# A two-layer decoder trunk on one core: the convolution's shifted copies are begun on GpSimd's queue instead of ScalarE's

## The chip, the cores and the metric

The kernel runs on one core of a Trainium2 chip. The core has five engines that run side by side, each with its own instruction queue worked off in order: TensorE (PE in the profile; its weight loads are PEld), VectorE (DVE), ScalarE (ACT), GpSimd (POOL) and SyncE (SP). ScalarE, GpSimd and SyncE can begin transfers (DMAs); the transfers themselves run on the core's 16 DMA engines. The metric is the device time of one execution in microseconds (us); lower is better.

## The reference, cut to what matters

Two decoder layers work on 256 tokens of 1024 numbers in float32. Layer 0 mixes a convolution group of 768 channels and a memory attention of 4 heads, then a dense SwiGLU; layer 1 mixes sliding-window attention and the memory attention, then 8 experts of which each token uses 2. The change lies in the convolution of layer 0:

```
a    = proj[..., :CONV_CH] + b_glu[:CONV_CH]
gate = proj[..., CONV_CH:2 * CONV_CH] + b_glu[CONV_CH:]
u = a * jax.nn.sigmoid(gate)
u_pad = jnp.pad(u, ((0, 0), (CONV_WIDTH - 1, 0), (0, 0)))
c = lax.conv_general_dilated(u_pad, dw_w[:, None, :], window_strides=(1,), padding='VALID',
    dimension_numbers=('NWC', 'WIO', 'NWC'), feature_group_count=CONV_CH) + dw_b
c = jax.nn.silu(layer_norm(c, ln_g, ln_b))
```

Each of the 768 channels is convolved along the tokens with its own 31 taps. The layer norm runs over all channels, so nothing behind it can start before the last channel is done.

## The kernel before, in words

The 768 channels are six blocks of 128 (c = 0 to 5). For each block TensorE makes the two halves of the input projection (`pa`, `pg`, lines 98 to 100), ScalarE the sigmoid (L393), VectorE the product `u` (L394), and ScalarE's queue writes `u` of the block to a DRAM buffer `ud` (L395).

The convolution is done on TensorE. A block's channels are cut into four groups of 32 (q = 0 to 3). For each group a transfer (L461) reads `ud` so that the 128 partitions of a tile `sh` hold 32 channels at four shifts of 0 to 3 tokens: 4 x 32 rows of 288 floats, 144 KB. GpSimd builds `bands` (L457), diagonal matrices of the taps, one buffer for each of two blocks in turn. Then 32 matmuls (8 tap groups g, each with q = 0, 1, 2, 3 in turn; L466) add up the block in the one PSUM buffer `pcv`, and ScalarE moves it to `cv` (L468). In the trace each of these matmuls is two records, so that x64 is a block.

`sh` has six buffers and a block takes four. So the first two copies of a block have buffers while the block before is still being multiplied, and the last two (q = 2, 3) can only be begun when the matmuls that read q = 0 and 1 of the block before are done. I call the start of such a pair a hand-over; there is one into each of blocks 1 to 5.

Between these stand other pieces of work that TensorE takes up meanwhile: the transposes `xt` and the matmuls `pkv` of the memory's keys and values, the memory query `pmq` (2 x 24 matmuls), transposes of heads `ht`, and the four rounds of memory attention: scores `sc`, softmax on VectorE and ScalarE (`nm`, `pr`), transposes `pt`, output `mo`. The heads are normed first: VectorE sums squares (`hss`), GpSimd makes the factor (`ms`, `rs`, lines 150 and 151), VectorE applies it (`kn`, `qn`), and TensorE's `ht` needs that. After block 5 come the layer norm (`pmean`, `pst`, `pbc`) and the output projection `wo`, and then the dense SwiGLU, layer 1 and the experts.

Weights are loaded on SyncE's queue into a small ring of buffers; a load begins when its buffer has been used up. The order of the instructions on each engine is worked out before the run by a scheduler that plays the program through with durations of its own, except for TensorE's order in the experts' stage, which is written out by hand. So a change of a transfer's queue can move instructions on other engines too.

```
sh = [wk0.tile([P, UW - 4], F32, name="sh", tag="sh", bufs=6) for _ in range(4)]
for q in range(4):
    act.dma_start(sh[q], bass.AP(tensor=ud.tensor, ...
```

Of the kernel before, what the change touches and what calls it, by code (L numbers as in the profile page):

```python
# [47 lines left out]
def hybrid_kernel(  # L48
# [7 lines left out]
    act, dve, pool, pe, sp = nc.scalar, nc.vector, nc.gpsimd, nc.tensor, nc.sync  # L56
# [81 lines left out]
    def col(name, k=0):  # L138
        return cols[:, offs[name] + k:offs[name] + k + 1]
# [27 lines left out]
    with ExitStack() as ph:  # L167
# [5 lines left out]
        def bank(tag, name):  # L173

            if tag in ("mm", "tp"):
                return psb.tile([P, 512], F32, name=name, tag=tag)
            return psx[-1].tile([P, 512], F32, name=name, tag=tag,
                                bufs=dict(sc=2, cv=1, o=1, acc=4, so=1)[tag])
# [167 lines left out]
        ud = dram.tile([NCT, P, UW], F32, name="ud")  # L346
# [35 lines left out]
        for i in range(3):  # L382
            wa, wg = [halves(m, pool if (i, j) in LOWPOOL else None, after=None)
                      for j, m in enumerate(win[2 * i:2 * i + 2])]
            for j in range(2):
                c = 2 * i + j
# [16 lines left out]
        for name, n, f in (("memg", KD, 32.0), ("ffg", KD, 32.0), ("swg", KD, 32.0),  # L403
                           ("hmk", 1, 8.0), ("hsk", 1, 8.0)):
            c = cols[:, offs[name]:offs[name] + n]
# [49 lines left out]
        for c in range(NCT):  # L455
            T = bands[:, c % 2]
            pool.tensor_tensor(T, eye4[:, None, None, :].to_broadcast([P, GT, 4, 32]),  # L457
                               w4[:, :, 4 * c:4 * c + 4, None].to_broadcast([P, GT, 4, 32]), op=OP.mult)
            sh = [wk0.tile([P, UW - 4], F32, name="sh", tag="sh", bufs=6) for _ in range(4)]
            for q in range(4):  # L460
                act.dma_start(sh[q], bass.AP(tensor=ud.tensor, offset=ud[c, 32 * q, 0:1].offset,  # L461
                                                  ap=[[1, 4], [UW, 32], [1, UW - 4]]))
            pcv = bank("cv", "pcv")[:, :S]
            for g in range(GT):
                for q in range(4):
                    pe.matmul(pcv[q * 32:(q + 1) * 32, :], T[:, g, q, :], sh[q][:, 4 * g:4 * g + S],  # L466
                              start=(g == 0), stop=(g == GT - 1), tile_position=(0, q * 32))
            act.activation(cv[:, c, :], pcv, AF.Identity, bias=col("dwb", c))  # L468
# [192 lines left out]
    with ExitStack() as ph:  # L661
# [99 lines left out]
        for kk in range(KD // 2):  # L761
# [6 lines left out]
            for k in range(2 * kk, 2 * kk + 2):  # L768
                q = k % 4
# [401 lines left out]
```

## Time and profile before

| what | value |
|---|---|
| median of 3 runs | 1364.86 us (1364.3 to 1366.51) |
| the profiled execution's own time | 1362.78 us |
| its span, first to last instruction | 1361.1 us |
| PE, PEld | 1286.2 us (94%), 720.4 us (53%) |
| DVE, ACT, POOL | 387.5 us (28%), 298.7 us (22%), 70.7 us (5%) |

Times in rows are microseconds from the span's start. The profiled execution is 1.7 us longer than its span and 2.08 us under the median. A row such as "[3.81 <-DMA sh<-ud]" says that the engine was idle for 3.81 us ahead of this instruction until a transfer into `sh` had landed. ACTq and SPq rows are the time that a queue spent on issuing a transfer, not the transfer itself. [...]

### The profile page before, as it was taken

What the parts mean: (1) busy time and instruction counts of PE and PEld (TensorE: products, weight loads), DVE (VectorE), ACT (ScalarE), POOL (GpSimd) and SP (SyncE); (2) the same over time, 40 slices, a digit from 0 to 9 for tenths busy, and PEclk for the clock granted to TensorE, in tenths of its full rate; (3) what the DMA queues carried; (4) which work ended last, traced back from release to release, by engine and by line L of the source; (5) the groups of instructions that cost most, each with busy time, mean ns of one, the idle gap of its engine ahead of it and who ended that gap; (6) DMA issues with size and microseconds to landing.
All of it is one profiled execution on the core that took longest, in us unless ns stands there. A gap on an engine that the chain in (4) does not pass through costs nothing. (4 is left out here: it accounts for less than half of the span.)

```text
span 1361.1 us, 19725 instructions
## 1 busy us (share of the span) xinstructions
PE 1286.2 (94%) x7908; PEld 720.4 (53%) x7908; DVE 387.5 (28%) x782; ACT 298.7 (22%) x575; POOL 70.7 (5%) x110
## 2 busy tenths in 40 slices
PE   6978799999898879999999999999999999999997
PEld 5844589999775643344454343444343454434443
DVE  5633465555466421012112111111110211100212
ACT  6333354444365300001111000011000111000111
POOL 4220200000031200000000000000000000000000
PEclk9989899999898988999999999999999999999999
DMA  9842145555472467989999999999999999999994
GB/s 291 291 132 72 63 149 198 184 184 184 124 223 83 191 230 299 363 336 394 413 409 409 409 412 404 409 410 412 409 409 404 411 409 408 412 411 409 403 411 199
DMA packets 137445, 420.87 MB, mean 309 GB/s; under 512 B 9658, under 2 KB 43256, under 8 KB 125048
## 3 DMA queue, kind: packets, MB, share of 16 engines
q1 hardware_dynamic: 133016, 414.39, 79.1%
q10 hardware_dynamic: 4320, 4.96, 1.1%
q8 instruction: 77, 1.26, 0.4%
q14 instruction: 32, 0.26, 0.1%
HBM read 417.37 MB, written 1.95 MB: 308 GB/s over the span
## 5 line engine op out<-in xcount | busy, mean ns | idle before, releaser
L926 PE MATMUL pa<-raw,xe 128*64 128x512 f32 x1024 | 269.8, 599 | 6.6 <-DVE hx L942 4.0
L926 PE MATMUL pb<-raw,xe 128*64 128x384 f32 x1024 | 213.2, 488 | 0.0
L982 PE MATMUL py<-raw,hT 128*64 128x512 f32 x896 | 199.3, 595 | 4.0 <-PEq L1023 1.6
L926 PEld LDWEIGHTS pb<-raw,xe 128*64 128x64 f32 x1024 | 81.1, 138 | 140.4 <-issue 140.4
L91 DVE TENSOR_TENSOR wlo<-raw,whi 128x1024 fp32r<-128x1024 f32 x108 | 131.9, 1260 | 80.8 <-ACT whi L90 80.8
L982 PEld LDWEIGHTS py<-raw,hT 128*64 128x64 f32 x896 | 67.5, 137 | 131.9 <-issue 121.4
L926 PEld LDWEIGHTS pa<-raw,xe 128*64 128x64 f32 x1024 | 77.5, 137 | 104.2 <-issue 70.0
L90 ACT CAST whi<-raw 128x1024 fp32r<-128x1024 f32 x112 | 111.5, 1046 | 54.5 <-issue 26.2
L934 PE MATMUL po<-raw,xe 128*32 128x512 f32 (+1 forms) x1024 | 116.3, 542 | 0.0
L975 DVE COPY hTo<-hto 128x224 f32<-128x224 f32 x32 | 12.5, 392 | 353.8 <-PE hto L973 353.8
L969 ACT COPY hT<-ht 128x448 f32<-128x448 f32 x32 | 17.1, 533 | 375.4 <-PE ht L967 375.4
L934 PEld LDWEIGHTS po<-raw,xe 128*32 128x32 f32 x1024 | 43.8, 109 | 55.2 <-issue 43.2
L992 PE MATMUL py<-raw,hTo 128*32 128x512 f32 x448 | 64.5, 594 | 3.3 <-PEq L1023 3.3
L942 DVE TENSOR_TENSOR hx<-s,pa 64x512 f32<-64x512 f32 x32 | 22.1, 690 | 152.6 <-ACT s L941 152.2
L958 DVE TENSOR_TENSOR hxo<-so,po 64x256 f32<-64x256 f32 x32 | 13.5, 423 | 156.8 <-ACT so L957 156.4
L941 ACT ACTIVATE s<-pa 64x512 f32<-64x512 f32 x32 | 18.9, 591 | 164.1 <-PE pa L926 163.8
L98 PE MATMUL fg<-xh,whi 128*128 128x256 f32 x176 | 50.2, 286 | 2.7 <-ACT fsg L557 2.5
L98 PE MATMUL fu<-xh,whi 128*128 128x256 f32 x176 | 50.1, 284 | 0.0
L99 PE MATMUL fu<-xh,wlo 128*128 128x256 f32 x176 | 50.1, 284 | 0.0
L100 PE MATMUL fg<-xl,whi 128*128 128x256 f32 x176 | 50.0, 284 | 0.0
L99 PE MATMUL fg<-xh,wlo 128*128 128x256 f32 x176 | 50.0, 284 | 0.0
L100 PE MATMUL fu<-xl,whi 128*128 128x256 f32 x176 | 49.9, 284 | 0.0
(297 smaller groups left out, 1620.4 us busy)
## 6 DMA issues: line engine op xcount, KB each, us to landing
raw<-in_sw_we_gate_dram SPq DMA_DIRECT2D x128, 896.0 KB
raw<-in_sw_we_up_dram SPq DMA_DIRECT2D x128, 896.0 KB
raw<-in_sw_we_down_dram SPq DMA_DIRECT2D x96, 1024.0 KB
raw<-in_sw_we_down_dram SPq DMA_DIRECT2D x32, 512.0 KB
raw<-in_cv_w_gate_dram SPq DMA_DIRECT2D x11, 1024.0 KB
raw<-in_cv_w_up_dram SPq DMA_DIRECT2D x11, 1024.0 KB
raw<-in_cv_w_down_dram SPq DMA_DIRECT2D x11, 1024.0 KB
raw<-in_cv_w_in_dram SPq DMA_DIRECT2D x7, 1024.0 KB
```

The costliest lines, as they stand in the source:

```text
L90: act.copy(hi[:, i:i + step], v[:, i:i + step])
L91: (low or dve).tensor_tensor(lo[:, i:i + step], v[:, i:i + step], hi[:, i:i + step].bitcast(F32), op=OP.subtract)
L98: pe.matmul(ps, ah, bh, start=first, stop=False)
L99: pe.matmul(ps, al, bh, start=False, stop=False)
L100: pe.matmul(ps, ah, bl, start=False, stop=last)
L926: pe.matmul(ps[half * HD:(half + 1) * HD, :c1 - c0], x, v[:, c0:c1], start=(k == 0), stop=(k == KD - 1), tile_position=(0, half * HD))
L934: pe.matmul(po[q * 32:(q + 1) * 32, :c1 - c0], x, v[:, k % 2, c0:c1], start=(k == 0), stop=(k == KD - 1), tile_position=(0, q * 32))
L941: act.activation(s[:HD, :], pa[:HD, :], AF.Silu)
L942: dve.tensor_tensor(hx[:HD, :], s[:HD, :], pa[HD:, :], op=OP.mult)
L969: act.copy(hT, b[:, :3 * P + HD])
L982: pe.matmul(py[n][n * HD:(n + 1) * HD, :], hT[:, o:o + HD], w[q // 2][:, q % 2, n * 512:(n + 1) * 512], start=(p == 0 and q == 0), stop=(p ...
L992: pe.matmul(py[n][r:r + 32, :], hTo[:, o:o + 32], w[q // 2][:, q % 2, n * 512:(n + 1) * 512], start=(i < 2), stop=(i >= NR * BLK - 2), til ...
```

## The change

The 24 transfers of L461 (six blocks of four) are begun on GpSimd's queue. Nothing else is edited.

```diff
             for q in range(4):
-                act.dma_start(sh[q], bass.AP(tensor=ud.tensor, offset=ud[c, 32 * q, 0:1].offset,
+                pool.dma_start(sh[q], bass.AP(tensor=ud.tensor, offset=ud[c, 32 * q, 0:1].offset,
                                                   ap=[[1, 4], [UW, 32], [1, UW - 4]]))
```

The scheduler then also places other instructions anew. On GpSimd, from the first transfers of block 2 on (`sh_1037` to `sh_1040` are block 2, `sh_1080` and `sh_1081` the first two of block 3; `ms_726` belongs to the keys of the first 128 tokens, `ms_741` to those of the other 128, `ms_791` to the first memory query):

```order
+L461 DMA sh_1037<-ud_171 128x1x288
 L457 TENSOR_TENSOR bands_949<-eye4_172,w4_182 128x1024
+L461 DMA sh_1038<-ud_171 128x1x288
 L150 TENSOR_SCALAR ms_726<-hss_724 128x4
 L151 TENSOR_TENSOR rs_727<-ms_726,neghalf_78 128x4
+L461 DMA sh_1039<-ud_171 128x1x288
+L461 DMA sh_1040<-ud_171 128x1x288
 L457 TENSOR_TENSOR bands_949<-eye4_172,w4_182 128x1024
+L461 DMA sh_1080<-ud_171 128x1x288
+L461 DMA sh_1081<-ud_171 128x1x288
 L150 TENSOR_SCALAR ms_741<-hss_739 128x4
+L150 TENSOR_SCALAR ms_791<-hss_789 128x4
```

GpSimd had only the bands and the heads' factors here; now the hand-over into block 2 (`sh_1039`, `sh_1040`) and two more transfers stand ahead of the factors of the second keys.

On TensorE, where block 2 meets the second half of the memory query:

```order
 L99 MATMUL pmq<-whi,xl 128x256
 L100 MATMUL pmq<-wlo,xh 128x256
-L466 MATMUL pcv<-sh,bands 32x256 x19
+L466 MATMUL pcv<-sh,bands 32x256 x32
 L239 MATMUL ht<-ident,kn 128x128 x2
```

Block 2 had 19 of its 32 matmuls ahead of the second keys' transposes; now it has all 32 there.

On TensorE, behind the second half of the memory query, where block 3 begins:

```order
-L466 MATMUL pcv<-sh,bands 32x256 x13
+L466 MATMUL pcv<-sh,bands 32x256 x2
 L251 MATMUL sc_840<-mkT,mqT 128x256
 L251 MATMUL sc_841<-mkT,mqT 128x256
 L466 MATMUL pcv<-sh,bands 32x256 x26
```

The last 13 matmuls of block 2 stood here, and block 3 began behind the first scores; now block 2 is over long before, and two matmuls of block 3 come first.

## Rows read from the trace of the kernel before

**Rows 1.** Busy time in stretches: PE, PEld, DVE, ACT, POOL, PEclk, DMA share, GB/s
```profile
52.00:84.00 32.00, 29.16 (x237) 19.13 (x236) 14.87 (x22) 14.50 (x26) 7.33 (x6) 1.00 0.77 230
84.00:110.00 26.00, 17.46 (x148) 8.94 (x148) 7.59 (x13) 5.89 (x11) 4.60 (x5) 0.80 0.37 101
560.00:1350.00 790.00, 780.06 (x4568) 336.66 (x4566) 120.02 (x283) 80.66 (x178) 0.00 (x0) 1.00 1.00 400
```

**Rows 2.** Who waited for whom, 28 to 150: total us, times, longest us
```profile
POOL bands L457 <- PE pcv L466: 42.9, 4, 20.4
...
PE pcv L466 <- DMA sh<-ud: 11.7, 7, 3.8
...
ACT sg L393 <- DMA ud<-u: 5.9, 1, 5.9
...
ACT xh L217 <- DMA sh<-ud: 3.6, 1, 3.6
```

**Rows 3.** TensorE in order of time: start, us, instruction, records, idle before
```profile
57.01 3.23 PE L466 MATMUL pcv<-sh,bands 128*32 128x256 f32 x56 [1.68 <-DMA sh<-ud]
...
79.78 0.36 PE L98 MATMUL pmq<-whi,xh 128*128 128x256 f32 x1
...
82.83 0.62 PE L466 MATMUL pcv<-sh,bands 128*32 128x256 f32 x4
...
87.26 1.04 PE L466 MATMUL pcv<-sh,bands 128*32 128x256 f32 x2 [3.81 <-DMA sh<-ud]
...
90.11 3.64 PE L466 MATMUL pcv<-sh,bands 128*32 128x256 f32 x32 [1.82 <-DMA sh<-ud]
...
93.69 0.64 PE L239 MATMUL ht<-ident,kn 128*128 128x128 f32 x2
...
103.00 0.62 PE L466 MATMUL pcv<-sh,bands 128*32 128x256 f32 x2 [2.30 <-DMA sh<-ud]
...
104.60 4.35 PE L466 MATMUL pcv<-sh,bands 128*32 128x256 f32 x46 [0.98 <-DMA sh<-ud]
...
124.27 1.13 PE L474 MATMUL pmean<-cv,ones 128*128 128x256 f32 x4
...
127.94 0.63 PE L466 MATMUL pcv<-sh,bands 128*32 128x256 f32 x6
```

**Rows 4.** All issues of L461: ns min/median/max, first and last start
```profile
L461 ACTq DMA_DIRECT2D sh<-ud x24: 514/516/2972, 41.1 to 124.6; - x24
```

**Rows 5.** ScalarE's queue in order of time, the issues of L461
```profile
62.74 3.92 ACTq L461 DMA_DIRECT2D sh<-ud  x3
...
79.08 0.52 ACTq L461 DMA_DIRECT2D sh<-ud  x1
...
80.06 3.15 ACTq L461 DMA_DIRECT2D sh<-ud  x3
...
98.88 0.52 ACTq L461 DMA_DIRECT2D sh<-ud  x1
...
99.46 0.51 ACTq L461 DMA_DIRECT2D sh<-ud  x1
...
123.98 0.51 ACTq L461 DMA_DIRECT2D sh<-ud  x1
```

**Rows 6.** Two stretches, columns as in Rows 1: copies alone, and copies beside loads
```profile
118.00:120.00 2.00, 2.00 (x26) 0.89 (x20) 0.00 (x0) 0.00 (x0) 0.00 (x0) 1.00 0.25 86
...
70.00:76.00 6.00, 5.77 (x31) 3.02 (x30) 2.31 (x3) 0.84 (x1) 0.00 (x0) 1.00 0.81 225
```

**Rows 7.** GpSimd in order of time
```profile
39.60 1.57 POOL L164 TENSOR_TENSOR rt<-ssum,neghalf 128x1 f32<-128x1 f32 x2 [1.82 <-DVE ssum L161]
...
79.54 2.83 POOL L457 TENSOR_TENSOR bands<-eye,w 128x1024 f32<-128x1024 f32 x1 [0.68 <-PE pcv L466]
82.45 0.24 POOL L150 TENSOR_SCALAR ms<-hss 128x4 f32<-128x4 f32 x1
82.77 1.04 POOL L151 TENSOR_TENSOR rs<-ms,neghalf 128x4 f32<-128x4 f32 x1
```

## The prediction

> **What bounds the kernel now.** I read the busy times by stretch first. From 560 us to the end TensorE is busy for 780.06 of 790 us and the DMA engines are full [rows 1]: the experts' stage leaves nothing to gain, and since every load there waits for a buffer that the work ahead frees, it starts later or earlier with that work. So a microsecond won or lost in the convolution should reach the end whole. The convolution lies between 40 and 135 us. Between 52 and 84 us TensorE has the full clock; between 84 and 110 us it is busy for 17.46 of 26 us, at a mean clock of 0.80 [rows 1]. So this is where time lies.
>
> Next the table of waits. TensorE's largest loss is the wait for the copies `sh`: 11.7 us in 7 pieces. ScalarE stands still for 5.9 and 3.6 us behind its own issues [rows 2], but TensorE has work in its queue meanwhile; I count nothing for these.
>
> The order in time gives the pieces: 1.68 us ahead of 57.01 (block 0), 3.81 + 1.82 us ahead of 87.26 and 90.11 (block 2), 2.30 + 0.98 us ahead of 103.00 and 104.60 (block 3) [rows 3]; these are 10.6 of the 11.7 us. The two larger pairs cost twice. [...] Against 58 ns that is 32 x 56 ns = 1.8 us and 46 x 37 ns = 1.7 us. After the short wait of 1.68 us there is no such loss [rows 3]. So 11.7 + 3.5 = 15.2 us is all that faster copies can give.
>
> Why are the copies late? The first of the pair into block 2 was begun at 79.08 and ended a wait at 87.26, 8.2 us later; the second was begun at 80.06 and ended one at 90.11, 10.0 us later. Into block 3 it took 98.88 to 103.00, 4.1 us, and 99.46 to 104.60, 5.1 us [rows 3, 5]. With copies alone under way the DMA share is 0.25 at 86 GB/s, so a copy keeps a quarter of the 16 engines, and 144 KB takes 1.7 us there. Beside weight loads the share is 0.81 [rows 6]. The slow pair had both the loads beside it and other copies ahead of it: three were issued from 62.74 on, none until 79.08 [rows 5].
>
> **The change part by part.** 24 issues leave ScalarE's queue and 24 come to GpSimd's. No transfer is added and no byte moved more.
>
> The price of one issue on GpSimd has no row. The ends are ScalarE's: 0.514 us at the shortest, 2.97 us at the longest, 0.516 us in the median [rows 4]. A landing has the ends 4.1 and 10.0 us. I take 1.0 us for an issue, near the shorter end because the long issues are few, and let a landing take 0.5 us longer than the quiet rows: 4.6 us for the first of a pair and 5.6 us for the second, each from its own start; at block 2, where loads run beside, 0.5 us more for the first.
>
> *Block 0.* GpSimd is done with its earlier work at 39.60 + 1.57 = 41.2 us [rows 7]. Four issues of 1.0 us end at 45.2; even the slowest landing, 10.0 us, comes to 54.2 for the last one begun at 44.2. TensorE asks at 57.01 - 1.68 = 55.3. The wait goes: -1.7 us, and all that follows is earlier by that.
>
> *Into block 2.* Its first two copies are now begun on GpSimd at about 60 and 64 us, behind block 0's matmuls, so they lie well ahead of the pair. The pair, behind block 1's matmuls as before, is begun at 79.08 - 1.7 = 77.4 and 78.4. The first lands at 77.4 + 5.1 = 82.5, the second at 78.4 + 5.6 = 84.0. TensorE gets there at 83.45 (82.83 + 0.62) - 1.7 = 81.7. So it waits 0.8 us and, with a couple of matmuls between, some 1.2 us more: 2.0 us instead of 5.63. -3.6 us.
>
> What stands behind these issues on GpSimd: `bands` of block 3, block 3's first two copies, then the factors of the second keys and the first query, which VectorE and then TensorE's `ht` wait for. In time: 77.4 + 2 x 1.0, + 2.83 for the bands, + 2 x 1.0, + 2 x (0.24 + 1.04) for the factors = 86.8 [rows 7]; 0.4 us of VectorE makes 87.2. TensorE does all 32 matmuls of block 2 first now and ends them at 84.0 + 29 x 0.117 = 87.4 (two records of 58 ns each). The factors are just hidden, by 0.2 us; each 1.0 us more per issue moves them by 4 and the matmuls by 1. That is the price if this cover goes.
>
> *Into block 3.* Before, 13 matmuls of block 2 stood behind the second half of `pmq`, so the pair was begun only at 98.88 and TensorE had little left: 2.30 + 0.98 us of wait. Now block 2 is over at 87.4; the pair is begun at 87.4 and 88.4 and lands at 92.0 and 94.0. TensorE has 24 matmuls `pmq` meanwhile, 3.0 us as from 79.78 to 82.83 [rows 3], two pairs of `ht` (0.6 us each by the row at 93.69), two matmuls of block 3 and two scores, some 2 us in all: it asks at 92.5 and waits 1.5 us. -1.8 us.
>
> *Into blocks 4 and 5.* Into block 4 the softmax work covers as much as before; the small wait stays: 0. Into block 5 there was no wait: the pair was begun from 123.98 on, and `pmean` and `wo` filled 124.27 to 127.94 [rows 3, 5], 3.7 us. With landings of 4.6 and 5.6 us that cover is short by 0.9 and then 0.6 us: +1.5 us. The remaining waits of under 0.3 us each: -0.2.
>
> Waits: -1.7 - 3.6 - 1.8 + 0 + 1.5 - 0.2 = -5.8 us. The waits that stay are no longer than 2.0 us, near the 1.68 us that was followed by full speed; so the 3.5 us at the lower clock go too. Sum: -9.3 us. On the profiled execution that is 1362.78 - 9.3 = 1353.5; this execution is 2.08 us under the median, so 1364.86 - 9.3 = 1355.6, said as 1356.
>
> [...]
>
> **The rivals.**
>
> *Only the issue moves.* If the landing is set by the DMA engines alone, the pair into block 2 again takes 8.2 and 10.0 us. Then only block 0's 1.7 us and the small 0.2 us are won: 1363. For it: the share of 0.25 is the same whoever begins the transfer, if each copy keeps its quarter. Against: the queue ahead of the pair is emptier, and 13 matmuls have moved to where they cover block 3's pair. [...]
>
> *The copies run side by side.* If the four copies of a block go over different quarters of the engines, a landing beside loads is no longer than a quiet one and four take 1.7 us together instead of 6.8. Then of the 15.2 us only about 2 us stay, at blocks 2 and 5: -13 us, 1352. For it: 0.25 with copies alone leaves three quarters free. Against: no row shows two copies side by side. [...]
>
> *Slower: GpSimd's queue becomes the chain.* If an issue costs 2.97 us there, the factors for the second keys come at 77.4 + 4 x 2.97 + 2.83 + 2.6 + 0.4 = 95.1, later than the 93.69 at which `ht` ran before [rows 3]. From there each hand-over is two issues long; block 3's last copy lands near 104, as before (104.60), block 4's I count at nothing, and into block 5, behind bands, two copies and its own pair, the last copy lands near 133 instead of 124.6 + 5.1 = 129.7 [rows 3 to 5]: +3.4 us, 1368. Between -9.3 at 1.0 us and +3.4 at 2.97 us the sign turns at about 2.4 us per issue. For it: nothing in the trace prices an issue on GpSimd, and a power of four numbers per partition takes 1.04 us there [rows 7]. Against: ScalarE's long issues fell where the DMA share was 0.77, and between 98 and 100 us, at a share of 0.37, they took 0.51 to 0.52 us [rows 1, 5].
>
> **How the numbers follow.** Forecast 0.50, side by side 0.25, only the issue moves 0.12, slower 0.13. No change means within 0.2%, 2.7 us, about what a measurement of this kernel can tell. The forecast's own range, with landings 1 us shorter or 2 us longer at three hand-overs, is 1352 to 1361. Faster: 0.50 + 0.25 = 0.75; same 0.12; slower 0.13. The range goes from 1349, just under the case in which all 15.2 us go (1349.7), to 1367, short of the slow case.
>
> **What would show it.** GpSimd's queue row for L461 should read about 1 us. The wait for `sh` at block 0 should be gone, the one at block 2 about 2 us, at block 3 about 1.5 us, and a new one before block 5. Convolution records at 58 ns behind them, and the mean clock of the stretch 84 to 110 near 1.0. `pmean` should come about 10 us before its old 124.27. I am wrong if issues take over 2.4 us, if `ht` waits for `rs`, if the pair's landing keeps its 8 to 10 us, or if the gain at `pmean` is there and lost later on.

## The result, and the profile after

The changed kernel takes 1350.78 us (median of 4 runs, 1349.67 to 1351.22); beside it the kernel before took 1365.68 us (4 runs, 1364.3 to 1367.58). The ratio is 0.9892 (95% interval 0.9877 to 0.9906), 14.9 us by the medians. The profiled execution took 1349.67 us, its span 1348.0 us against 1361.1 us; these 13.1 us are less than 14.9 because the profiled execution of before was 2.9 us under its median and this one 1.1 us. The forecast was 1356 us, with a range of 1349 to 1367.

The busy times by stretch answer to [rows 1]. TensorE is now busy for 23.59 instead of 17.46 us between 84 and 110 us, and PEclk, the granted share of its full clock, is 1.00 there instead of 0.80.

```profile
52.00:84.00 32.00, 30.81 (x245) 20.00 (x243) 14.93 (x21) 14.28 (x25) 11.33 (x15) 1.00 0.89 252
84.00:110.00 26.00, 23.59 (x251) 13.55 (x255) 11.91 (x27) 11.75 (x29) 12.35 (x14) 1.00 0.42 115
```

The table of waits from 28 to 150 us answers to [rows 2]: TensorE's wait for `sh` has fallen from 11.7 us in 7 pieces to 2.0 us in 2. GpSimd now stands still ahead of its issues, waiting for TensorE to give the buffers back; no row shows another engine that loses by it.

```profile
PE pcv L466 <- DMA sh<-ud: 2.0, 2, 1.4
POOL sh L461 <- PE pcv L466: 24.2, 5, 13.0
```

TensorE in order of time answers to [rows 3]. The two waits stand ahead of block 2. Its remaining 58 records take 3.64 / 58 = 63 ns each, where 32 took 114 ns; the granted clock is 1.00 (85.0 to 88.7 us), where it was 0.50 (90.1 to 93.8 us). Block 3 (92.04, 93.23) has no wait in TensorE's own rows.

```profile
81.75 0.62 PE L466 MATMUL pcv<-sh,bands 128*32 128x256 f32 x4
82.97 0.62 PE L466 MATMUL pcv<-sh,bands 128*32 128x256 f32 x2 [0.59 <-DMA sh<-ud]
85.03 3.64 PE L466 MATMUL pcv<-sh,bands 128*32 128x256 f32 x58 [1.44 <-DMA sh<-ud]
...
92.04 0.63 PE L466 MATMUL pcv<-sh,bands 128*32 128x256 f32 x4
...
93.23 3.92 PE L466 MATMUL pcv<-sh,bands 128*32 128x256 f32 x52
...
102.32 0.72 PE L279 MATMUL pt<-ident,pr 128*128 128x128 f32 x4 [1.17 <-DVE pr L274]
...
110.75 1.13 PE L474 MATMUL pmean<-cv,ones 128*128 128x256 f32 x4
```

TensorE's weight loads (PEld) wait for `sh` too, and their rows show what is left at blocks 3 and 5: 0.57 and 0.62 us.

```profile
93.94 2.73 PEld L466 LDWEIGHTS pcv<-sh,bands 128*32 128x32 f32 x50 [0.57 <-DMA sh<-ud]
...
116.04 1.02 PEld L466 LDWEIGHTS pcv<-sh,bands 128*32 128x32 f32 x24 [0.62 <-DMA sh<-ud]
```

All issues of L461 answer to [rows 4], and GpSimd in order of time to [rows 7]. An issue takes 0.68 us in the median and never over 1.12 us. From issue to landing it is 6.3 us in the median of all 24. The long ones are among the first ten copies, issued by 63.8 us, for which TensorE never waits; the pairs into blocks 2 to 5 land after 3.9 to 5.9 us. The pair into block 2 is begun at 78.27 us, that into block 3 at 88.56.

```profile
L461 POOL DMA_DIRECT2D sh<-ud x24: 677/679/1122, 41.7 to 111.4; - x24
...
DMA to landing us min/median/max: 3.7/6.3/13.6
```

```profile
78.27 1.45 POOL L461 DMA_DIRECT2D sh<-ud  x2 [0.48 <-PE pcv L466]
79.73 1.93 POOL L457 TENSOR_TENSOR bands<-eye,w 128x1024 f32<-128x1024 f32 x1
81.59 1.37 POOL L461 DMA_DIRECT2D sh<-ud  x2
83.03 0.54 POOL L150 TENSOR_SCALAR ms<-hss 128x4 f32<-128x4 f32 x2
83.64 2.03 POOL L151 TENSOR_TENSOR rs<-ms,neghalf 128x4 f32<-128x4 f32 x2
88.56 1.46 POOL L461 DMA_DIRECT2D sh<-ud  x2 [2.89 <-PE pcv L466]
```

One window sums it up: from block 0's first matmul to `pmean` (columns as in [rows 1]). The first row is the kernel before, where the first six records of block 0 began at 54.60 us, ahead of the wait of 1.68 us; the second is the kernel after.

```profile
54.60:124.27 69.67, 56.94 (x478) 31.63 (x477) 28.37 (x48) 26.21 (x54) 13.84 (x12) 0.93 0.50 146
```

```profile
55.28:110.75 55.47, 51.87 (x477) 30.69 (x476) 24.29 (x46) 23.77 (x51) 23.70 (x29) 1.00 0.65 182
```

TensorE's idle time falls from 12.7 to 3.6 us and its busy time, with the clock now full throughout, by 5.1 us: 14.2 us together. Block 0 itself began 0.7 us later than before (over all ten traces it begins between 53.64 and 55.28 us), so `pmean` comes 13.5 us earlier. The first matmul of layer 1's projection (`pin`) comes 13.5 us earlier (355.7 instead of 369.2), the experts' first gather (`ga`) 13.6 us (469.0 instead of 482.6), the end 13.1 us. Nothing is lost on the way.

### The profile page after: what moved, and what is told of

It reads as the page before. It is cut to its first block, busy times and chain, and to the rows that moved or that the text cites. A ratio compares the mean times of both kernels' runs of the same rounds, so it can differ in the third digit from the quotient of the medians.

```text
span 1348.0 us, 19743 instructions
## 1 busy us (share of the span) xinstructions
PE 1282.6 (95%) x7908; PEld 721.9 (54%) x7908; DVE 385.7 (29%) x782; ACT 298.9 (22%) x575; POOL 86.2 (6%) x134
## 5 line engine op out<-in xcount | busy, mean ns | idle before, releaser
L958 DVE TENSOR_TENSOR hxo<-so,po 64x256 f32<-64x256 f32 x32 | 13.5, 423 | 156.9 <-ACT so L957 156.6
```

## The experiments

The line numbers of some runs are shifted by their edits. Three explanations were open. A: it is enough to leave ScalarE's queue. B: GpSimd's transfers land sooner beside the weight loads. C: the new order of TensorE's instructions carries the gain. Later D: the copies land late since each keeps to a quarter of the DMA engines.

**Another queue** (`e1_sp`).

```diff
-                pool.dma_start(sh[q], ...
+                sp.dma_start(sh[q], ...
```

> The 24 copies are begun on SyncE's queue instead of GpSimd's. Theory A (leaving ScalarE's queue is what counts; the landing doesn't depend on who begins the copy): about as after, 1351 to 1354 us. Theory B (a copy begun on GpSimd travels in larger packets and so gets a larger share beside the weight loads; other queues move it as ScalarE's does): the pair into block 2 still takes 8 to 10 us to land, TensorE waits there for about 5 us, 1358 to 1366 us. Theory C (the new order of TensorE's instructions is what counts): this kernel has 19 + 13 matmuls of block 2 as before, so it should keep block 3's wait and stay above 1356 us.

Measured: 1370.17 us, ratio to before 1.0033 (1.0019 to 1.0047). A falls. Block 3 keeps its wait (2.05 + 1.37 us), as C said. But B, as I put it, was too strong: the pair into block 2 was begun at 78.62 and ended waits at 84.25 and 86.46, 5.6 and under 8 us, and TensorE waited 2.86 us there, not 5. The loads of the layers' weights are issued on the same queue, and stood behind the copies:

```profile
78.62 2.86 SPq L461 DMA_DIRECT2D sh<-ud  x4
81.57 1.35 SPq L77 DMA_DIRECT2D raw<-in_cv_w_down_dram  x1
```

**The new queue with the old order** (`e2_old_order`; `pq` is the memory query's last matmul).

```diff
+                        if c == 2 and 4 * g + q >= 19:
+                            late.enter_context(tc.issue_after(pq.ins))
                         pe.matmul(pcv[q * 32:(q + 1) * 32, :], T[:, g, q, :], ...
```

> The copies are begun on GpSimd, but the last 13 matmuls of block 2 are held behind the memory query's last matmul, as they stood before the change. Theory C (order): the wait into block 3 comes back at 2.5 to 3.3 us, with some 1.7 us of half clock behind it: 1354 to 1356 us. Theory B (landings alone): the wait into block 3 is under 1.5 us and the clock stays: 1351 to 1352 us.

Measured: 1364.54 us, ratio to before 0.9995 (0.9983 to 1.0007): the whole gain is gone, more than either theory said.

```profile
81.43 0.62 PE L469 MATMUL pcv<-sh,bands 128*32 128x256 f32 x2 [0.72 <-DMA sh<-ud]
83.53 3.56 PE L469 MATMUL pcv<-sh,bands 128*32 128x256 f32 x32 [1.49 <-DMA sh<-ud]
...
96.28 0.62 PE L469 MATMUL pcv<-sh,bands 128*32 128x256 f32 x2 [2.08 <-DMA sh<-ud]
...
98.46 3.63 PE L469 MATMUL pcv<-sh,bands 128*32 128x256 f32 x28 [0.67 <-DMA sh<-ud]
```

Block 2's waits are as in the kernel after (2.2 us). Block 3's come back (2.75 us), as C said, with records of 3.63 / 28 = 130 ns behind them, at a granted clock of 0.50 (98.64 to 103.64 us). But behind block 2's waits, too, a record takes 111 ns, at 0.52 (83.5 to 87.0 us); after nearly the same waits the changed kernel ran at 1.00. From block 0's first matmul to `pmean` it is 65.20 us (53.64 to 118.84): of the 14.2 us only 4.5 are left. The rest of the loss lies far behind and is told below.

**Fewer loads beside the copies** (`e3_act_quiet`; `gate_ins` is block 2's last matmul).

```diff
+            with tc.issue_after(gate_ins):
+                lg, lu = [load_rows(m[0][:, i * 256:(i + 1) * 256], KD) for m in (cv_w_gate, cv_w_up)]
```

> The kernel before, but the first gate and up weights of the dense SwiGLU are loaded only behind block 2's matmuls, so fewer loads run beside the copies of blocks 1 and 2. Theory B (the loads slow the copies): the pair into block 2 lands in 4 to 6 us instead of 8 to 10, TensorE's 5.6 us of wait there falls to about 2, and 4 to 5.5 us are won: 1360 to 1362 us, if the late loads cost nothing. Rival (the queue of ScalarE itself delays them): the wait stays above 4.5 us and the time at about 1365 us or above.

Measured: 1364.42 us, 0.9992 (0.998 to 1.0005). The edit did not do what the expectation says. Block 2's last matmul ends at 98.4 us, and the first two gate and up loads had long begun:

```profile
59.57 0.37 SPq L77 DMA_DIRECT2D raw<-in_cv_w_gate_dram  x1
62.78 0.37 SPq L77 DMA_DIRECT2D raw<-in_cv_w_up_dram  x1
...
69.14 0.37 SPq L77 DMA_DIRECT2D raw<-in_cv_w_gate_dram  x1
74.16 0.37 SPq L77 DMA_DIRECT2D raw<-in_cv_w_up_dram  x1
```

In the kernel before they began at 58.57, 61.82, 66.51 and 72.33 us, as early. Every engine has the same instructions in the same order as before. So this is the kernel before a second time, and neither theory was tested. That ScalarE's copies move more slowly beside loads rests on the views of the transfers further below: 0.39 MB in 9 us with loads, 0.26 MB in 3 us with hardly any.

As a repeat it shows how far two traces of one and the same kernel differ:

```profile
58.22 4.92 PE L466 MATMUL pcv<-sh,bands 128*32 128x256 f32 x56 [1.89 <-DMA sh<-ud]
...
86.12 0.62 PE L466 MATMUL pcv<-sh,bands 128*32 128x256 f32 x2 [0.34 <-DMA sh<-ud]
89.55 3.47 PE L466 MATMUL pcv<-sh,bands 128*32 128x256 f32 x32 [2.81 <-DMA sh<-ud]
```

The pair into block 2, begun at 81.41 and 82.41, ended waits after 4.7 and 7.1 us instead of 8.2 and 10.0, and those waits were 3.15 us instead of 5.63. Block 0 waited 0.17 + 1.89 us instead of 1.68, and the records behind that took 4.92 / 56 = 88 ns instead of 58; the mean granted clock from 52 to 84 us was 0.95 instead of 1.00. From block 0's first matmul to `pmean` it is 70.6 us instead of 69.7. So a single wait can differ by over 2 us from trace to trace, the whole stretch differs by 1 us here. I therefore compare the kernels by this stretch.

**Another list for the same bytes** (`e4_act_wide`).

```diff
-                                                  ap=[[1, 4], [UW, 32], [1, UW - 4]]))
+                                                  ap=[[UW, 32], [1, 4], [1, UW - 4]]))
```

> The kernel before, but each copy lists its 32 channels first and the four shifts inside, so that its rows are dealt out in another way; taps and channels then meet in other pairs, so the convolution's values are not the reference's, the work is the same. Rival theory D (a copy is slow because its four shifts of 32 rows each keep it on a quarter of the engines): the DMA share of a copy alone rises well over 0.25, landings fall by 1 us or more, and much of the 14.9 us is won: 1353 to 1359 us. Theory B (small packets beside large ones): the packets stay small, so the pair into block 2 still takes over 7 us, 1362 to 1366 us.

The total (1384.29 us) says nothing, which I had not foreseen: other values send other tokens to the experts, whose `po` matmuls rose from 1024 to 1280 records. Up to there the run is comparable: `pmean` came at 107.9 us instead of 124.3 and `pin` at 351.2 instead of 369.2, on ScalarE's queue and in the order of before. D's gain is there, and larger than it said. It is run with the right taps below.

**The old queue with the new order** (`e5_act_new_order`).

```diff
+            if c == 2:
+                with tc.issue_after(mmc.ins):
+                    query(1)
```

> The copies stay on ScalarE's queue, but the second half of the memory query is held behind block 2's last matmul, so that TensorE meets blocks 2 and 3 in nearly the order that it has after the change. Theory C (the order alone carries the gain): the wait into block 3 and the half clock behind it go, pmean comes 8 us or more earlier than the 124.3 us of before, 1353 to 1358 us. Theory B (a copy begun on GpSimd lands sooner beside loads, and that alone carries it): the waits into block 2 stay at 5 to 6 us and so does most of the time, 1361 to 1366 us. Theory BC (both are needed, since the order comes to nothing if the half clock behind block 2's long wait stays): between them, 1358 to 1361 us.

Measured: 1365.18 us, 0.9997 (0.9984 to 1.0011).

```profile
86.34 1.06 PE L465 MATMUL pcv<-sh,bands 128*32 128x256 f32 x2 [2.00 <-DMA sh<-ud]
90.48 3.24 PE L465 MATMUL pcv<-sh,bands 128*32 128x256 f32 x32 [3.08 <-DMA sh<-ud]
...
101.36 3.64 PE L465 MATMUL pcv<-sh,bands 128*32 128x256 f32 x58 [0.44 <-DMA sh<-ud]
```

The order does its part at block 3 (a wait of 0.44 us instead of 3.28), the queue's part stays (5.08 us at block 2), and block 4 now waits for 1.74 us. From block 0's first matmul to `pmean` it is 65.2 us (54.76 to 119.94). The four cases of queue and order: 69.7 us with neither, 65.2 with the queue, 65.2 with the order, 55.5 with both. Singly they give 4.5 us each, together 14.2: the other 5.2 come only with both. In this stretch the mean clock is 0.93 with neither, 0.92 in either single case, and 1.00 with both. `pmean` came 4.3 us earlier than before and not 8, so the order alone does not carry the gain; without the 6.4 us that this run lost later (below) its total would be some 1359 us, in BC's range. Against this kernel the changed one has another queue and nearly the same order (here 13 matmuls of block 2 still stand behind the second keys' transposes), and it is 9.7 us shorter.

**The spread list, on either queue** (`e6_act_spread`, `e7_pool_spread`). Beside the list, the taps are brought into the same order:

```diff
+            tq = cv[:96, 1, q * P:(q + 1) * P]
+            dve.tensor_copy(tq.rearrange("r (n j) -> r j n", j=4), taps[q].rearrange("r (j n) -> r j n", j=4))
```

> The kernel before, on ScalarE's queue, with each copy's 32 channels as the outer list, and with the taps brought into the same order by two small copies on VectorE, so that the convolution is the reference's. Theory D (four shifts as the outer list keep a copy on a quarter of the DMA engines, and that is why it lands late; who begins it is second): the copies land within 3 to 4 us, the waits for them fall under 1.5 us in all, pmean comes at 107 to 110 us, 1348 to 1351 us. Theory B (only GpSimd's transfers do well beside loads): 1360 us or above.

> The same spread list as in the run before it, but begun on GpSimd's queue. Theory D: once the copy is spread, the queue is worth under 2 us either way, 1347 to 1352 us. Theory B (GpSimd's own way of moving the copy counts beside it): better than the spread copies on ScalarE by 2 us or more, at or under 1347 us.

Measured: 1345.45 us on ScalarE's queue, ratio to before 0.9857 (0.9838 to 0.9876), and 1344.55 us on GpSimd's, 0.9853 (0.9834 to 0.9873). Both beat the changed kernel, and both lie below the ranges that D gave. In `e6_act_spread` TensorE has the order of before, 19 and 13 matmuls of block 2, and waits 0.8 us in all; from block 0's first matmul to `pmean` it takes 53.0 us instead of 69.7, with the same queue and order. So the list alone removes these waits, as D expected. `e7_pool_spread` has the order of the kernel after and no wait for `sh` left; it takes 51.3 us. What GpSimd's queue and that order add to the spread list is thus 0.9 us by the medians and 1.7 us by this stretch, under the 2 us that B asked for.

The views of the transfers show why. Of each kernel one stretch: the share of each queue (the last column) is that of all 16 engines; q10 is ScalarE's queue, q0 GpSimd's, q1 SyncE's, which brings the loads. First the kernel before, with loads beside (69 to 78 us) and with hardly any (88 to 91 us):

```profile
DMA packets 2056, 2.12 MB, mean 236 GB/s; under 512 B 40, under 2 KB 2055, under 8 KB 2055
...
q1 hardware_dynamic: 1702, 1.71, 69.5%
q10 hardware_dynamic: 353, 0.39, 15.4%
```

```profile
DMA packets 234, 0.26 MB, mean 88 GB/s; under 512 B 10, under 2 KB 232, under 8 KB 234
...
q10 hardware_dynamic: 229, 0.26, 23.8%
q1 hardware_dynamic: 5, 0.01, 0.7%
```

The kernel after, from 64 to 68 us with loads beside:

```profile
DMA packets 786, 0.81 MB, mean 203 GB/s; under 512 B 341, under 2 KB 688, under 8 KB 786
...
q0 software_dynamic: 428, 0.46, 57.5%
q1 hardware_dynamic: 358, 0.36, 54.6%
```

And from 47 to 48 us, with hardly any loads:

```profile
q0 software_dynamic: 138, 0.19, 116.6%
q1 hardware_dynamic: 9, 0.02, 11.5%
```

The spread list on ScalarE's queue, from 109 to 110.2 us, copies alone:

```profile
DMA packets 260, 0.27 MB, mean 226 GB/s; under 512 B 25, under 2 KB 260, under 8 KB 260
...
q10 hardware_dynamic: 260, 0.27, 71.3%
```

A share is the time that packets took, and packets can overlap: from 47 to 48 us one queue alone has 116.6%. Before, copies alone stay at a quarter (23.8%, 88 GB/s) though three were issued together, and beside loads they bring 0.39 MB in 9 us: the copies issued at 62 us are still under way when the pair into block 2 is begun (from 78 to 79 us this queue still moved 0.04 MB). GpSimd's fill 57.5% beside loads, more than twice the 23.8%, and bring 0.46 MB in 4 us, 115 GB/s; with hardly any loads they brought 0.19 MB in 1 us. Both are more than ScalarE's copies reached alone, which fits several copies side by side. Spread, the copies on ScalarE's queue fill 71.3% at 226 GB/s. The views give a queue's share of all 16 engines, not which of them a copy used: that the old list kept ScalarE's copies to one and the same quarter, and that GpSimd's lay on different ones, is an estimate from 23.8, 57.5 and 71.3%. There is a second difference: a copy's packets hold 4.6 KB on GpSimd's queue (98 of them from 64 to 68 us) and 1.15 KB on ScalarE's (342 from 69 to 78 us); of the 341 packets under 512 bytes above, 279 hold 16 bytes and come with GpSimd's transfers. No run separates what the larger packets do beside loads from what the spread does; with the spread list on ScalarE's queue, packets of 1.15 KB were no hindrance to 226 GB/s.

**Only the pairs on GpSimd** (`e8_pool_pair_only`).

```diff
+                (pool if q > 1 else act).dma_start(sh[q], ...
```

> Only the last two copies of each block (q = 2 and 3, those of a hand-over) are begun on GpSimd, the first two stay on ScalarE's queue. TensorE's order changes again: 3 matmuls of block 2, then the second half of the memory query, then 27. Theory B: the pairs land in 4 to 6 us as after, so 1350 to 1356 us, depending on the cover. Rival (the four copies of a block hold each other up on the quarter of the engines, whoever begins them): the pair into block 2 takes 7 us or more to land, 1356 to 1364 us.

Measured: 1367.48 us, 1.0029 (1.0014 to 1.0043), above both ranges, though some 6.5 us of it were lost later (below). The pair into block 2 lands soon, as B said (begun at 80.40, in use at 84.93). But block 0's first two copies are ScalarE's again (2.80 us of wait), and in the order that the scheduler made of it blocks 3 and 4 wait for 2.57 and 2.88 us.

**What four of the runs lost later.** In `e1_sp`, `e2_old_order`, `e5_act_new_order` and `e8_pool_pair_only` the time from layer 1's `pin` to `ga` is 119.8 to 120.4 us; in the other six it is 113.1 to 113.6. These four have one and the same order of TensorE's instructions in layer 1's attention, and the other six another, though no line there was edited. Some rows of it, - as before, + as in the four:

```
-MATMUL pt<-ident,pr 128x128
-MATMUL ht<-ident,qn 128x128 x3
-MATMUL pt<-ident,pr 128x128 x3
-MATMUL mo<-pT,mv 64x128 x4
+MATMUL pt<-ident,pr 128x128 x4
```

In the second order the mean granted clock falls to 0.67 and 0.65 over 20 us of that attention, here in `e2_old_order`: about two thirds of the time, if the lower level is the 0.50 seen behind block 3's waits. At the same place the kernel before holds 1.00 (429.2 to 449.2 us).

```profile
424.90:434.90 10.00, 9.49 (x43) 5.04 (x41) 7.90 (x32) 6.02 (x26) 0.94 (x5) 0.67 0.01 2
434.90:444.90 10.00, 10.00 (x35) 5.54 (x35) 3.81 (x12) 3.18 (x11) 0.37 (x2) 0.65 0.00 0
```

So the totals of these four hold 6.4 to 7.0 us that were lost behind the convolution, and the verdicts above rest on `pmean` and `pin`. From block 0's first matmul to `pmean` they take 67.7, 65.2, 65.2 and 67.8 us (69.7 before, 55.5 after). By `pin` (369.2 us before, 355.7 after) they stand at 370.9, 364.9, 365.1 and 366.2 us, and the two spread kernels at 353.4 and 350.9. That the order is the cause of the later loss rests on ten of ten traces that go together; no run changed this order alone.

## Why the prediction was right, and where it was short

*The end.* That what is won in the convolution reaches the end whole: 13.5 us at `pmean`, 13.1 in the span. Right, but on a condition that I had not stated: layer 1's order stayed the same. Four experiments show that this was not certain; here the forecast had luck.

*Block 0.* -1.7 us, as worked out; the wait is gone. The block began 0.7 us later, though, so that it was over 1.3 us earlier.

*Into block 2.* Forecast 2.0 us of wait, measured 0.59 + 1.44 = 2.03. The landings were near enough as well: 82.97 - 78.27 = 4.7 us to the end of the first wait (5.1 assumed); the second was forecast for 84.0 and came at 85.0. The factors for the second keys (`rs`) ended at 85.67 and block 2 at 88.67; with 0.4 us of VectorE the cover was 2.6 us, not 0.2: the four issues took 2.8 us and not 4, the bands 1.9 and not 2.83, and block 2 ended 1.3 us later than forecast. The wait of before against which 3.6 us were counted, 5.63 us, was itself 3.15 us in the second trace of that kernel (`e3_act_quiet`).

*Into blocks 3, 4 and 5.* Here the sizes were off. Forecast were 1.5 us left at block 3, the 0.84 us of block 4 kept, and 1.5 us new at block 5; TensorE's rows show no wait at any of them, the weight loads' 0.57 and 0.62 us. That is 3.8 us of the 4.2 by which 13.5 exceeds 9.3. The term that was mis-sized is the landing, "0.5 us longer than the quiet rows"; no row or run shows these 0.5 us for the pairs of blocks 3 to 5. The pairs of blocks 3, 4 and 5 landed 3.9 and 4.6, 4.4 and 4.2, 4.1 and 4.6 us behind their issues, where I had 4.6 and 5.6. The second copies landed 1.0 to 1.4 us sooner than that. The second of block 3, begun at 89.3 (half of 1.46 us behind 88.56), was in use at 93.94.

*The clock.* Forecast -3.5 us, from records of 3.23 / 56 = 58 ns behind 57.01, 3.64 / 32 = 114 ns behind 90.11 and 4.35 / 46 = 95 ns behind 104.60 [rows 3], with a granted clock of 1.00, 0.50 and 0.64 there; measured -5.1 us of busy time. Right in the result, but the reason (waits of up to 2 us are followed by full speed) doesn't hold: in `e2_old_order` waits of 0.72 and 1.49 us at the same place were followed by 111 ns per record, and in `e3_act_quiet` 0.17 and 1.89 us at block 0 by 88 ns, while `e8_pool_pair_only` kept a granted clock of 1.00 (52 to 84 us; 3.65 / 60 = 61 ns) behind 2.80 us there. The changed kernel was lucky.

*Against it.* The wait for the softmax grew from 0.47 to 1.17 us, which I had at nothing.

*The rivals.* That only the issue moves is refuted by the kernel with the new order on ScalarE's queue: 65.2 against 55.5 us, 9.7 us between two kernels that also differ a little in order. With the spread list 0.9 to 1.7 us are left. GpSimd's queue as the chain would have needed 2.4 us per issue; it was 0.68. The rival of copies side by side (1352 us, to which I gave 0.25) is the one that the transfers bear out (57.5% and 115 GB/s on GpSimd's queue beside loads, 23.8% and 88 GB/s on ScalarE's alone), and 1350.78 us lies nearer to it than to the forecast's 1356. The forecast took its landings from ScalarE's quiet rows, in which the copies together have a share of 0.25 [rows 6]. It still had the larger part of the gain, because the waits at blocks 0 and 2, the new order's cover of block 3 and the clock were in its sum.

## What to carry to other kernels

Copies that were alone had a DMA share of 0.25 here, and of 0.71 when the outermost number of their list was 32 instead of 4: where a trace shows such a share, try the list before moving the transfer to another queue. Here the queue, with the order that came with it, gave 14.9 us by the medians, and the list 19.7 us on the old queue. Where a scheduler places the instructions, compare variants by milestones (a first matmul of each stage), not by totals: an edit can turn the order of a stage 300 us further on, which here was worth about half of the change. And look at the trace whether an edit did what it was meant to, before its result is read.

## What the runs showed of the hardware that was not expected

The same copy's issue costs very different times: three on ScalarE's queue took 3.92 us [rows 5], while its earlier copies were still moving, and four on SyncE's 7.46 us in `e1_sp`, while none on GpSimd's took over 1.12 us; with the spread list ScalarE's took 0.52 to 0.73 us. And the length of an idle time did not tell whether the granted clock falls: 0.59 + 1.44 us ahead of block 2 left it at 1.00 in the changed kernel (85.0 to 88.7 us), 0.72 + 1.49 us were followed by 0.52 in `e2_old_order` (83.5 to 87.0 us); at block 0, 2.80 us left it at 1.00 in `e8_pool_pair_only` (52 to 84 us), 0.17 + 1.89 us were followed by records of 88 ns in `e3_act_quiet`, at 0.95 in the mean of the same 32 us.
